# Token forms on VectorE, range sums on ScalarE, and another set of blocks in pairs, in a one-core decoder step on Trainium2

## The chip, the cores and the metric

The kernel runs on 1 core of one Trainium2 chip. A core has TensorE (PE in the profile; its weight loads are PEld), VectorE (DVE), ScalarE (ACT), GpSimd (POOL) and SyncE (SP), each with its own queue that it works off in order. Data come from HBM by DMA. The metric is the device time in microseconds of one execution, as the median of several; a profiled execution beside them gives the trace.

## The reference

One layer of a hybrid decoder is applied to 264 token columns (256 of a prompt, 8 single new tokens): a SwiGLU with half weight, a mixing block, a second SwiGLU, a last norm.

```
h = h + 0.5 * swiglu(rmsnorm(h, norm_ffn1), ffn1_gate, ffn1_up, ffn1_down)
mix = mixing_block(rmsnorm(h, norm_mix), w_in, ..., w_out, states)   # mLSTM heads | gated convolution
h = h + mix
h = h + 0.5 * swiglu(rmsnorm(h, norm_ffn2), ffn2_gate, ffn2_up, ffn2_down)
y = rmsnorm(h, norm_final)

def swiglu(x, wg, wu, wd):
    return (jax.nn.silu(x @ wg) * (x @ wu)) @ wd
```

`D_MODEL` is 2048 and `D_FF` 5504; all inputs are float32. Outputs are y and the new states of the mixing block.

## The kernel before

**Layout and precision.** Activations lie with channels on the 128 partitions and the 264 tokens along the row; 2048 channels are 16 blocks of 128, and 5504 are 43, split into a half 0 of 22 and a half 1 of 21. Every float32 operand is cut into a high and a low part of float16. ScalarE writes the high part (`high`, line 241), VectorE the low part (`low`, line 249). A regular product (`three`, lines 323 to 325) takes three matmuls of 264 columns for each 128x128 weight block: high by high, high by low, low by high.

**Weights.** `fetch` issues the DMA of a tile of up to 8 blocks (`wraw`), cuts its high part at once and its low part right away or, in the feed-forward parts (`lag`), with the next fetch. At most 5 tiles are cut ahead of TensorE.

**Pairs.** Some products are made two at a time (`product_pair`): gate and up of one block (key `gu`, table `GU_SEVEN`), or two columns of the down product (key `dd`, table `DOWN_SEVEN`). High by high stays as it is (line 387, 264 columns). The two correction terms are made in seven products of half the tokens (132 columns, lines 371 and 372) where eight would be needed. For that the kernel needs sums of weights (`weight_sums`, line 302, VectorE, four for each two tiles) and sums and differences of token halves, the "forms" (`token_sums`, line 359): `f` of the norm's output for gate/up, `g` of the activations for down. Before, GpSimd makes them, 4 instructions for two 128-channel blocks. Three banks of PSUM are joined afterwards (`join`, lines 427 to 437): ScalarE copies one piece, VectorE does the rest.

**What follows.** In gate/up, VectorE scales the result by the norm, ScalarE does SiLU, VectorE multiplies, and both cut the activation (`activated`). In the down products VectorE adds to h (line 872, or 855 for a joined pair). In half 1, `done` follows for each finished column: the next norm's cut (`xm`, both engines) and its square (GpSimd) in layer 1, the square and the last gain (line 919, ScalarE) in layer 2.

**Watching the range.** The float16 form is valid only for values in a range. `watch` (line 568) sums the absolute values of the last 16 columns of each regular product, on VectorE; a pair has its own sum (line 437). At the end a verdict is formed from them (`judge`), and a second, float32 form of the program would run if it failed.

**Order.** The schedule is written out by hand. `tick` counts products in halves, and `at(delta, fn)` puts work off by so many; what is put off stands in the engines' queues where its tick comes.

Of the kernel before, what the change touches and what calls it, by code (L numbers as in the profile page):

```python
# [8 lines left out]
F32 = mybir.dt.float32  # L9
# [3 lines left out]
AF = mybir.ActivationFunctionType  # L13
ALU = mybir.AluOpType
# [5 lines left out]
T = SEQ + NS  # L20
DFF = 5504
NFB = DFF // 128
HALVES = (range(0, 22), range(22, NFB))
# [5 lines left out]
WK = 8  # L29
# [7 lines left out]
SEEN = 16  # L37
# [13 lines left out]
GU_SEVEN = {  # L51
    n: [j for half in starts for j in half]
    for n, starts in (
        ("1", (range(7, 22, 5), range(9, 22, 5), range(22, NFB - 1, 5), range(24, NFB - 1, 5))),
        ("2", (range(5, 22, 5), range(7, 22, 5), range(22, NFB - 1, 5), range(24, NFB - 1, 5))),
    )
}
DOWN_SEVEN = {("1", 0): (1, 3, 5, 7), ("1", 1): (1, 3, 5, 6), ("2", 0): (1, 3, 5, 7), ("2", 1): (1, 3, 4)}
PAIRS = sum(len(v) for v in GU_SEVEN.values()) + sum(len(v) for v in DOWN_SEVEN.values())
TH = T // 2  # L60

# [104 lines left out]
def step(ctx: ExitStack, tc: tile.TileContext, a: dict, shared, bad=None):  # L166
    nc = tc.nc
    ident, beyond = shared
    PSUM = bass.MemoryType.PSUM
    half_size = bad is not None  # L170
    PART = F16 if half_size else F32R
# [4 lines left out]
    side = nc.gpsimd if half_size else nc.vector  # L176
# [12 lines left out]
    for kb in range(0, KB, 4):  # L189
        t = hpool.tile([128, 4, T], F32, name=f"h{kb}", tag=f"h{kb}")  # L190
# [104 lines left out]
    beside, sums, spool = [], [], [None]  # L295
# [12 lines left out]
    def at(delta, fn, *args):  # L308
        agenda.setdefault(int(seq[0]) + delta, []).append((fn, args))
# [37 lines left out]

    def token_sums(out, even, odd):  # L350

        left, right = slice(0, TH), slice(TH, T)
        for n, x, y, op in (
            (0, odd[:, :, left], odd[:, :, right], ALU.subtract),
            (1, even[:, :, right], odd[:, :, right], ALU.subtract),
            (2, out[:, 0], even[:, :, right], ALU.add),
            (3, even[:, :, left], out[:, 2], ALU.subtract),
        ):
            side.tensor_tensor(out[:, n], x, y, op=op)  # L359

    def product_pair(key, x, forms, order):

# [199 lines left out]
    def watch(ps, rows=None):  # L562

        if half_size:
            j, n = len(stats), ps.shape[-1]
            stats.append(j)
            for r in rows or [slice(0, 128)]:
                nc.vector.tensor_reduce(
                    stat[r, j : j + 1], ps[r, n - SEEN : n], axis=mybir.AxisListType.X,
                    op=ALU.add, apply_absolute_value=True,  # L570
                )

    def watch_norm(ssum):
# [102 lines left out]
    class Norm:  # L676


        def __init__(self, tag, col):
            self.tag, self.col, self.x, self.acc = tag, col, [None] * KB, None  # L680
            self.forms = []

        def block(self, kb):
            self.cut(kb)
            self.square(kb)

        def cut(self, kb):
            x = xpool.tile([128, 2, T], PART, tag=f"x{kb}", name=f"x{self.tag}{kb}")
            gain = gains[:, self.col + kb : self.col + kb + 1]
            if half_size and self.col == V_N1 and kb == 0:  # L690

                nc.vector.tensor_scalar(
                    x[:, 0, :], h[0], vecs[:, self.col : self.col + 1], sx, op0=ALU.mult,
                    op1=ALU.mult,
                )
                nc.vector.tensor_scalar_mul(gains, vecs[:, :V_FIN], sx)
                low(x[:, 1, :], h[0], x[:, 0, :], gain)
            else:
                split(x, h[kb], gain)
            self.x[kb] = x  # L700
            return x

        def form(self, k):
            t = self.fpool.tile([128, 4, 2, TH], PART, tag=f"f{k}", name=f"f{k}")
            token_sums(t, self.x[2 * k], self.x[2 * k + 1])
            self.forms.append(t)

        def square(self, kb):
            new = self.acc is None
# [7 lines left out]
        def square_pairs(self, pool, pairs):  # L717

            for i in pairs:
                sq = pool.tile([128, 2, T], F32, tag=f"f{i}", name=f"sq{i}")  # L720
                nc.scalar.activation(sq, hpair[i], AF.Square)
                if i == 0:
                    self.acc = sq
                elif half_size and i == 4:
                    self.more = sq
                elif half_size and i == 5:

                    side.tensor_tensor(self.more, self.more, sq, op=ALU.add)
                else:
                    nc.vector.tensor_tensor(self.acc, self.acc, sq, op=ALU.add)  # L730
                if half_size and i == KB // 2 - 1:
                    nc.vector.tensor_tensor(self.acc, self.acc, self.more, op=ALU.add)
# [25 lines left out]
    def ffn(layer, norm, done, start=None, end=None):  # L758
        with ExitStack() as stack:
# [11 lines left out]

            def activated(j, i, zu, sg):
                nc.vector.tensor_tensor(zu, zu, sg, op=ALU.mult)
                if i % 2 == 0:
                    couple[0] = apool.tile([128, 2, 2, T], PART, tag=f"a{i}", name=f"a{i}")
                act[j] = t = couple[0][:, i % 2]
                high(t[:, 0, :], zu, sa[layer])
                rest = t[:, 1, :], zu, t[:, 0, :], sa[layer]
                if lag[0] and j < blocks[-1] - 2:
                    at(1.5, low, *rest)  # L780
                else:
                    low(*rest)
                if half_size and i % 2:
                    at(2, act_form, i // 2, couple[0])

            couple, act_forms = [None], {}

            def act_form(n, pair):
                act_forms[n] = t = spool[0].tile([128, 4, 2, TH], PART, tag=f"g{n}", name=f"g{n}")
                token_sums(t, pair[:, 0], pair[:, 1])  # L790

            def by_seven(j, i):
                z, rest = join(product_pair((layer, "gu", j), norm.x, norm.forms, range(KB)))
# [14 lines left out]
            for half, blocks in enumerate(HALVES):  # L808
# [18 lines left out]
                for i, j in enumerate(blocks):  # L827
                    if j in sevens:
                        by_seven(j, i)
                        continue  # L830
                    if first and start is not None:

                        ps4 = start()
                        for n, ps in enumerate(ps4):
                            early[n // 2, "gu"[n % 2]] = ps
                        for step, pairs in ((0, (0, 1)), (1, (2, 3)), (1.5, (4, 5)), (2, (6, 7))):
                            at(step, norm.square_pairs, fpool, pairs)
                        tick(0)
                        for which in "gu":
                            early[2, which] = product((layer, which, 2), norm.x, range(KB))  # L840
                    if half_size and j == (3 if start is not None else 1):
                        for k in range(8):
                            at(1 + k / 2, norm.form, k)
                    lag[0] = half_size and j >= (3 if start is not None else 1)
                    if (j, "g") in early and not first:

                        at(j / 2 + 1, block, i, j)
                        continue
                    block(i, j)
# [3 lines left out]
                def joined(half, db, z, rest):  # L853
                    rest()
                    nc.vector.scalar_tensor_tensor(
                        hpair[db // 2], z, scale, hpair[db // 2], op0=ALU.mult, op1=ALU.add
                    )
                    if half == 1:
                        done(db)
                        done(db + 1)  # L860
                    if db // 2 == DOWN_SEVEN[layer, half][0]:
                        watch_tokens(z, 2 * (layer == "2") + half)

                for db in range(0, KB - apart, 2):
                    if half_size and db // 2 in DOWN_SEVEN[layer, half]:
                        forms = [act_forms[n] for n in range(len(blocks) // 2)]
                        ps = product_pair((layer, "dd", half, db), act, forms, list(blocks))
                        at(1, joined, half, db, *join(ps))
                        continue
                    for i in (db, db + 1):  # L870
                        ps = product((layer, "d", half, i), act, list(blocks))
                        nc.vector.scalar_tensor_tensor(
                            h[i], ps, scale, h[i], op0=ALU.mult, op1=ALU.add
                        )
                        if half == 1:
                            done(i)
                        watch(ps)
# [43 lines left out]
    def done(kb):  # L921
        nf.square(kb)
        gained(kb, slice(0, T))
# [767 lines left out]
```

## Time and profile before

| | |
|---|---|
| median of 3 runs | 1815.19 us (1814.66 to 1815.21) |
| the profiled execution | 1814.18 us, span 1812.5 us |
| granted TensorE clock | 0.997 |
| busy: PE, PEld | 1790.2 us, 1595.6 us |
| busy: DVE, ACT, POOL | 1535.5 us, 886.3 us, 402.5 us |
| moved by DMA | 381.48 MB, mean 210 GB/s |
| down products of layer 1, half 1 | 577 to 692 us |
| down products of layer 2, half 1 | 1683 to 1800 us |

A timeline row gives the start and the length in us, the engine, the line, what is written and read, and in brackets the engine's idle time before it and what ended that. A group row ends with busy time, the mean of one in ns, and the idle time before. A row of a stretch gives its two ends, its length and the busy time of PE, PEld, DVE, ACT and POOL, each with its count of instructions, then the clock, the DMA share and GB/s.

### The profile page before, as it was taken

How to read it: one execution, taken by the hardware profiler on the slowest of the kernel's cores; microseconds unless marked ns; L12 is line 12 of the kernel's file. 1: busy time of each engine (PE TensorE's matmuls, PEld its weight loads, DVE VectorE, ACT ScalarE, POOL GpSimd, SP SyncE). 2: the span in 40 equal slices, each digit the busy share in tenths (PEclk: the TensorE clock that was granted, in tenths of full speed). 3: DMA queues.
4: the chain of work that ended last, by engine and by line, in shares of the span. 5: the costliest groups of instructions: out<-in, count | busy, mean ns of one | idle time of the engine just before them, and what ended most of it. 6: DMA issues, size and time to landing. Idle time of an engine off the chain costs nothing.

```text
span 1812.5 us, 44544 instructions
## 1 busy us (share of the span) xinstructions
PE 1790.2 (99%) x18612; PEld 1595.6 (88%) x18612; DVE 1535.5 (85%) x2485; ACT 886.3 (49%) x1306; POOL 402.5 (22%) x432
## 2 busy tenths in 40 slices
PE   9999999999999999999999999999999999999997
PEld 7889988989998988888888888889989898898886
DVE  8999978888987998788888766889988898988685
ACT  7445444444444444667566645444444444444443
POOL 1921220011212122222121025612130001212221
PEclk9999999999999999999999999999999999999999
DMA  8666665666666556888887655666666666666554
GB/s 301 189 212 204 192 216 188 211 202 207 192 196 194 189 169 208 299 300 265 278 280 244 221 180 184 201 203 214 189 203 207 194 204 203 205 198 196 183 175 121
DMA packets 118514, 381.48 MB, mean 210 GB/s; under 512 B 14972, under 2 KB 24796, under 8 KB 118304
## 3 DMA queue, kind: packets, MB, share of 16 engines
q1 hardware_dynamic: 109104, 350.53, 60.4%
q0 software_dynamic: 8256, 27.57, 4.4%
q8 instruction: 147, 2.41, 0.5%
q14 instruction: 63, 0.52, 0.1%
q10 hardware_dynamic: 944, 0.45, 0.1%
HBM read 366.72 MB, written 11.78 MB: 209 GB/s over the span
## 4 chain that ended last, share of the span: by engine, by line
PE 90%; DVE 6%; DMA 1%; ACT 1%; issue 1%; POOL 0%; SPq 0%; DVEq 0%; ACTq 0%
PE ps L323 21%; PE ps L325 21%; PE ps L324 21%; PE ps L387 9%; PE ps L371 8%; PE ps L372 8%; DVE w L249 3%; DVE s L302 1%; DMA wraw<-in_w1gu 1%; ACT w L241 1%; PE ps L673 0%; PE ps L1360 0%; DMA h<-in_xt 0%; PE ps L1303 0%; ACT xm L241 0%
## 5 line engine op out<-in xcount | busy, mean ns | idle before, releaser
L249 DVE SCALAR_TENSOR_TENSOR w<-wraw,w 128x1024 f16<-128x1024 f32 (+3 forms) x692 | 829.1, 1223 | 92.4 <-ACT w L241 91.9
L241 ACT ACTIVATE w<-wraw 128x1024 f16<-128x1024 f32 (+3 forms) x692 | 670.1, 1007 | 204.0 <-PE ps L325 95.0
L323 PE MATMUL ps<-x,w 128*128 128x264 f16 x1760 | 485.8, 276 | 0.0
L324 PE MATMUL ps<-x,w 128*128 128x264 f16 x1760 | 485.8, 276 | 0.0
L325 PE MATMUL ps<-x,w 128*128 128x264 f16 x1760 | 485.8, 276 | 0.0
L325 PEld LDWEIGHTS <-w 128*128 128x128 f16 x3684 | 360.5, 98 | 54.7 <-DVE w L249 2.0
L324 PEld LDWEIGHTS <-w 128*128 128x128 f16 x3684 | 360.4, 98 | 54.0
L323 PEld LDWEIGHTS <-w 128*128 128x128 f16 x3684 | 360.8, 98 | 52.9 <-issue 0.6
L359 POOL TENSOR_TENSOR g<-a 128x264 f16<-128x264 f16 x84 | 109.7, 1325 | 827.9 <-DVE a L249 660.4
L323 PE MATMUL ps<-xm,w 128*128 128x264 f16 x896 | 247.3, 276 | 0.0
L325 PE MATMUL ps<-xm,w 128*128 128x264 f16 x896 | 247.3, 276 | 0.0
L324 PE MATMUL ps<-xm,w 128*128 128x264 f16 x896 | 247.3, 276 | 0.0
L325 PE MATMUL ps<-a,w 128*128 128x264 f16 (+2 forms) x772 | 204.4, 270 | 1.4 <-DVE w L249 1.4
L323 PE MATMUL ps<-a,w 128*128 128x264 f16 (+2 forms) x772 | 204.5, 270 | 0.0
L324 PE MATMUL ps<-a,w 128*128 128x264 f16 (+2 forms) x772 | 204.5, 270 | 0.0
L387 PEld LDWEIGHTS <-w 128*128 128x128 f16 x1574 | 151.4, 98 | 24.1 <-ACT w L241 2.9
L372 PEld LDWEIGHTS <-s 128*128 128x128 f16 x1560 | 151.8, 97 | 0.0
L371 PEld LDWEIGHTS <-s 128*128 128x128 f16 x1560 | 150.7, 97 | 0.1
L302 DVE TENSOR_TENSOR s<-s,w 128x1024 f16<-128x1024 f16 (+2 forms) x206 | 145.2, 705 | 3.6
L302 DVE TENSOR_TENSOR s<-w 128x1024 f16<-128x1024 f16 (+2 forms) x206 | 139.9, 720 | 4.1
L372 PEld LDWEIGHTS <-w 128*128 128x128 f16 x1184 | 115.8, 98 | 6.1 <-DVE w L249 4.4
L371 PEld LDWEIGHTS <-w 128*128 128x128 f16 x1184 | 115.5, 98 | 1.7
(271 smaller groups left out, 2335.5 us busy)
## 6 DMA issues: line engine op xcount, KB each, us to landing
wraw<-in_w2gu SPq DMA_DIRECT2D x172, 512.0 KB, 4.8
wraw<-in_w1gu SPq DMA_DIRECT2D x164, 512.0 KB, 4.7
wraw<-in_win SPq DMA_DIRECT2D x112, 512.0 KB, 5.6
wraw<-in_w2d SPq DMA_DIRECT2D x46, 448.0 KB, 3.9
wraw<-in_w1d SPq DMA_DIRECT2D x40, 512.0 KB, 4.5
wraw<-in_w2d SPq DMA_DIRECT2D x36, 512.0 KB, 4.5
wraw<-in_w1d SPq DMA_DIRECT2D x40, 448.0 KB, 4.0
wraw<-in_wout SPq DMA_DIRECT2D x32, 512.0 KB, 4.6
```

The source lines that it names most:

```text
L241: nc.scalar.activation(dst, src, AF.Copy, scale=scale)
L249: nc.vector.scalar_tensor_tensor(dst, src, scale, hi, op0=ALU.mult, op1=ALU.subtract)
L302: nc.vector.tensor_tensor(s[:, out], x, y, op=ALU.add)
L323: nc.tensor.matmul(ps, wh, xk[:, 0, :], start=first, stop=False)
L324: nc.tensor.matmul(ps, wh, xk[:, 1, :], start=False, stop=False)
L325: nc.tensor.matmul(ps, wl, xk[:, 0, :], start=False, stop=last)
L359: side.tensor_tensor(out[:, n], x, y, op=op)
L371: nc.tensor.matmul(ps, w[0], x[:, 1], start=first, stop=False)
L372: nc.tensor.matmul(ps, w[1], x[:, 0], start=False, stop=last)
L387: nc.tensor.matmul(ps[:, :T], hi[:, i], xs[i][:, 0], start=(k0 + i == 0), stop=False)
```

## The change

There are four edits. The tables change: gate/up pairs are every second block (35, before 29), and a half 1 has one down pair fewer in each layer (13 in all, before 15). `token_sums` runs on VectorE and takes eight blocks, four pairs, in one call of 4 instructions; for that x, the activations and the forms lie in tiles of eight blocks. `watch` runs on ScalarE as an Abs with a sum, into a scratch tile. And behind a joined down pair in half 1, `done` comes half a step and a whole step later, in place of at once.

```diff
 GU_SEVEN = {
...
-        ("1", (range(7, 22, 5), range(9, 22, 5), range(22, NFB - 1, 5), range(24, NFB - 1, 5))),
-        ("2", (range(5, 22, 5), range(7, 22, 5), range(22, NFB - 1, 5), range(24, NFB - 1, 5))),
+        ("1", (range(7, 21, 2), range(22, NFB - 1, 2))), ("2", (range(5, 21, 2), range(22, NFB - 1, 2))),
...
-DOWN_SEVEN = {("1", 0): (1, 3, 5, 7), ("1", 1): (1, 3, 5, 6), ("2", 0): (1, 3, 5, 7), ("2", 1): (1, 3, 4)}
+DOWN_SEVEN = {("1", 0): (1, 3, 5, 7), ("1", 1): (1, 3, 5), ("2", 0): (1, 3, 5, 7), ("2", 1): (1, 3)}
...
-    def token_sums(out, even, odd):
+    def token_sums(out, x):
...
-        for n, x, y, op in (
-            (0, odd[:, :, left], odd[:, :, right], ALU.subtract),
-            (1, even[:, :, right], odd[:, :, right], ALU.subtract),
-            (2, out[:, 0], even[:, :, right], ALU.add),
-            (3, even[:, :, left], out[:, 2], ALU.subtract),
+        even, odd = (x.rearrange("p (n e) s t -> p e n s t", e=2)[:, e] for e in (0, 1))
+        for n, a_, b_, op in (
+            (0, odd[:, :, :, left], odd[:, :, :, right], ALU.subtract),
+            (1, even[:, :, :, right], odd[:, :, :, right], ALU.subtract),
+            (2, out[:, 0], even[:, :, :, right], ALU.add),
+            (3, even[:, :, :, left], out[:, 2], ALU.subtract),
         ):
-            side.tensor_tensor(out[:, n], x, y, op=op)
+            nc.vector.tensor_tensor(out[:, n], a_, b_, op=op)
...
-                nc.vector.tensor_reduce(
-                    stat[r, j : j + 1], ps[r, n - SEEN : n], axis=mybir.AxisListType.X,
-                    op=ALU.add, apply_absolute_value=True,
+                seen = tmp.tile([128, SEEN], F32, tag="seen", name="seen", bufs=2)
+                nc.scalar.activation(
+                    seen[r], ps[r, n - SEEN : n], AF.Abs, accum_out=stat[r, j : j + 1]
                 )
...
-        def form(self, k):
-            t = self.fpool.tile([128, 4, 2, TH], PART, tag=f"f{k}", name=f"f{k}")
-            token_sums(t, self.x[2 * k], self.x[2 * k + 1])
-            self.forms.append(t)
+        def form(self, g):
+            t = self.fpool.tile([128, 4, 4, 2, TH], PART, tag=f"f{g}", name=f"f{g}")
+            token_sums(t, self.groups[g])
+            self.forms += [t[:, :, i] for i in range(4)]
...
-                if half_size and i % 2:
-                    at(2, act_form, i // 2, couple[0])
...
+                n = len(blocks) // 2 * 2
+                if half_size and i in (WK - 1, 2 * WK - 1, n - 1):
+                    at(2, act_form, g, groups[g][:, : min(WK, n - WK * g)])
...
-                        for k in range(8):
-                            at(1 + k / 2, norm.form, k)
+                        for g in range(2):
+                            at(1 + g, norm.form, g)
...
                     if half == 1:
-                        done(db)
-                        done(db + 1)
+                        at(0.5, done, db)
+                        at(1, done, db + 1)
```

How the queues change is shown at two places. The first is VectorE in layer 1, half 1, from the scaling of a regular block's up product (`tc`) to the join of the pair that follows it (`y`); `a` are activations, `w` weight cuts, `g` forms. Before, at blocks 28 (regular) and 29 (pair):

```order
L823 TENSOR_TENSOR tc<-ps,rstd 128x264
L773 TENSOR_TENSOR tc<-tc,tb 128x264
L568 TENSOR_REDUCE stat<-ps 128x1
L249 SCALAR_TENSOR_TENSOR w<-wraw,w 128x1024 x2
L249 SCALAR_TENSOR_TENSOR a_6148<-y_6319,a_6148 128x264
L249 SCALAR_TENSOR_TENSOR a_6468<-tc,a_6468 128x264
L249 SCALAR_TENSOR_TENSOR w<-wraw,w 128x1024 x2
L430 TENSOR_TENSOR y_6645<-y_6645,ps 128x132
```

Now, at blocks 29 (regular) and 30 (pair), where eight blocks of activations are complete:

```order
L837 TENSOR_TENSOR tc<-ps,rstd 128x264
L780 TENSOR_TENSOR tc<-tc,tb 128x264
L248 SCALAR_TENSOR_TENSOR w<-wraw,w 128x1024 x2
L248 SCALAR_TENSOR_TENSOR a_5621<-y_6506,a_5621 128x264
L248 SCALAR_TENSOR_TENSOR a_5621<-tc,a_5621 128x264
L248 SCALAR_TENSOR_TENSOR w<-wraw,w 128x1024
L359 TENSOR_TENSOR g_6751<-a_5621 128x1056 x2
L359 TENSOR_TENSOR g_6751<-g_6751,a_5621 128x1056
L359 TENSOR_TENSOR g_6751<-a_5621,g_6751 128x1056
L248 SCALAR_TENSOR_TENSOR w<-wraw,w 128x1024
L430 TENSOR_TENSOR y_6833<-y_6833,ps 128x132
```

The reduction is gone, and once in eight blocks four instructions of 1056 elements stand between two weight cuts, ahead of the next join.

The second place is ScalarE in layer 1, half 1, at the joined down pair of columns 10 and 11 (`y` is the join's copy, `xm` the next norm's input, `seen` the range sum). Before:

```order
L427 COPY y_9908<-ps 128x132
L241 ACTIVATE xm_9917<-h_82,gains 128x264
L241 ACTIVATE xm_9923<-h_82,gains 128x264
L241 ACTIVATE w<-wraw 128x640
L241 ACTIVATE w<-wraw 128x896 x5
L427 COPY y_10153<-ps 128x132
```

Now:

```order
L427 COPY y_10001<-ps 128x132
L240 ACTIVATE w<-wraw 128x896
L240 ACTIVATE xm_9667<-h_82,gains 128x264
L240 ACTIVATE w<-wraw 128x896 x2
L240 ACTIVATE xm_9667<-h_83,gains 128x264
L569 ACTIVATE seen,stat<-ps 128x16
L240 ACTIVATE xm_9667<-h_82,gains 128x264
L240 ACTIVATE w<-wraw 128x896 x3
```

A weight cut now stands ahead of the pair's first `xm`, two more ahead of its second, and a range sum follows the regular product of columns 12 and 13; before, that product was a pair as well.

More of the change, by code (lines that the diff above doesn't have):

```diff
@@ L680, in __init__ @@
             self.tag, self.col, self.x, self.acc = tag, col, [None] * KB, None
-            self.forms = []
+            self.forms, self.groups = [], []
         def block(self, kb):
@@ L687, in cut @@
         def cut(self, kb):
-            x = xpool.tile([128, 2, T], PART, tag=f"x{kb}", name=f"x{self.tag}{kb}")
+            g, i = kb // WK, kb % WK
+            if i == 0:
+                self.groups.append(
+                    xpool.tile([128, WK, 2, T], PART, tag=f"x{g}", name=f"x{self.tag}{g}")
+                )
+            x = self.groups[g][:, i]
             gain = gains[:, self.col + kb : self.col + kb + 1]
@@ L719, in square_pairs @@
             for i in pairs:
-                sq = pool.tile([128, 2, T], F32, tag=f"f{i}", name=f"sq{i}")
+                if i % 4 == 0:
+                    self.four = pool.tile([128, 4, 2, T], F32, tag=f"f{i // 4}", name=f"sq{i}")
+                sq = self.four[:, i % 4]
                 nc.scalar.activation(sq, hpair[i], AF.Square)
@@ L773, in activated @@
                 nc.vector.tensor_tensor(zu, zu, sg, op=ALU.mult)
-                if i % 2 == 0:
-                    couple[0] = apool.tile([128, 2, 2, T], PART, tag=f"a{i}", name=f"a{i}")
-                act[j] = t = couple[0][:, i % 2]
+                g = i // WK
+                if i % WK == 0:
+                    groups[g] = apool.tile(
+                        [128, min(WK, len(HALVES[0]) - i), 2, T], PART, tag=f"a{g}", name=f"a{g}"
+                    )
+                act[j] = t = groups[g][:, i % WK]
                 high(t[:, 0, :], zu, sa[layer])
@@ L782, in activated, with act_form @@
                     low(*rest)
-                if half_size and i % 2:
-                    at(2, act_form, i // 2, couple[0])
[L786 to L790, printed above, removed]
+                n = len(blocks) // 2 * 2
+                if half_size and i in (WK - 1, 2 * WK - 1, n - 1):
+                    at(2, act_form, g, groups[g][:, : min(WK, n - WK * g)])
+            groups, act_forms = {}, {}
+            def act_form(g, x):
+                n = x.shape[1] // 2
+                room = min(WK, len(HALVES[0]) - WK * g) // 2
+                t = spool[0].tile([128, 4, room, 2, TH], PART, tag=f"g{g}", name=f"g{g}")[:, :, :n]
+                token_sums(t, x)
+                act_forms[g] = [t[:, :, i] for i in range(n)]
             def by_seven(j, i):
@@ L865, in ffn @@
                     if half_size and db // 2 in DOWN_SEVEN[layer, half]:
-                        forms = [act_forms[n] for n in range(len(blocks) // 2)]
+                        forms = [x for g in range(3) for x in act_forms[g]]
                         ps = product_pair((layer, "dd", half, db), act, forms, list(blocks))
```

## The prediction

> **What bounds the kernel now.** I read the page first, then TensorE's timeline and its waits, then the queues of ScalarE and VectorE around each wait.
>
> ```profile
> span 1812.5 us, 44544 instructions
> PE 1790.2 (99%) x18612; PEld 1595.6 (88%) x18612; DVE 1535.5 (85%) x2485; ACT 886.3 (49%) x1306; POOL 402.5 (22%) x432
> PE 90%; DVE 6%; DMA 1%; ACT 1%; issue 1%; POOL 0%; SPq 0%; DVEq 0%; ACTq 0%
> ```
>
> TensorE is busy 99%, but the page says that a matmul's end is modelled, so the price of a matmul has to come from starts. These are the starts in layer 1, half 1: block 27 (a pair), block 28 (regular), block 29 (a pair).
>
> ```profile
> 408.80 1.96 PE L387 MATMUL ps<-x,w 128*128 128x264 f16 x16
> 410.60 0.22 PE L371 MATMUL ps<-x,w 128*128 128x132 f16 x1
> ...
> 413.82 1.96 PE L387 MATMUL ps<-x,w 128*128 128x264 f16 x16
> ...
> 418.84 0.28 PE L323 MATMUL ps<-x,w 128*128 128x264 f16 x1
> ...
> 429.64 1.96 PE L387 MATMUL ps<-x,w 128*128 128x264 f16 x16
> 434.66 1.96 PE L387 MATMUL ps<-x,w 128*128 128x264 f16 x16
> ```
>
> 16 matmuls of 264 columns take 410.60 - 408.80 = 1.80 us, 112.5 ns each; the 56 of 132 columns after them take 413.82 - 410.60 = 3.22 us, 57.5 ns each. The pair takes 10.04 us (408.80 to 418.84), the regular block 10.80 us (418.84 to 429.64). So TensorE is bound by its own stream here, and what it does not spend there it loses at a few places:
>
> ```profile
> 673.59 0.29 PE L372 MATMUL ps<-a,w 128*128 128x264 f16 x1 [3.25 <-DVE w L249]
> 674.88 0.40 PE L372 MATMUL ps<-a,w 128*128 128x264 f16 x1 [0.32 <-DVE w L249]
> 1751.73 0.74 PE L387 MATMUL ps<-a,w 128*128 128x264 f16 x5 [2.62 <-ACT w L241]
> 1755.18 0.29 PE L325 MATMUL ps<-a,w 128*128 128x264 f16 x1 [0.37 <-DVE w L249]
> 1772.90 0.29 PE L325 MATMUL ps<-a,w 128*128 128x264 f16 x1 [1.01 <-DVE w L249]
> ```
>
> All five lie in the down products of a half 1. The first two are in the pair of columns 12 and 13 of layer 1, the third in the pair of columns 8 and 9 of layer 2, the last two just behind that one. They add up to 7.57 us of idle time. A matmul's modelled 0.276 us overlaps its successor by 0.276 - 0.1125 = 0.16 us, which the idle time does not count, so the loss is nearer to 7.57 + 5 x 0.16 = 8.4 us. Why they happen stands in the other queues:
>
> ```profile
> 659.67 0.27 ACT L427 COPY y<-ps 128x132 f32<-128x132 f32 x1 [0.19 <-PE ps L372]
> 670.44 0.92 ACT L241 ACTIVATE xm<-h,gains 128x264 f16<-128x264 f32 x2 [10.51 <-DVE h L855]
> 671.27 4.08 ACT L241 ACTIVATE w<-wraw 128x640 f16<-128x640 f32 x5
> 1738.32 0.27 ACT L427 COPY y<-ps 128x132 f32<-128x132 f32 x1 [0.36 <-PE ps L372]
> 1749.13 0.52 ACT L919 ACTIVATE h<-h,vecs 128x264 f32<-128x264 f32 x1 [10.54 <-POOL sq L711]
> 1750.95 4.92 ACT L241 ACTIVATE w<-wraw 128x640 f16<-128x640 f32 x6
> 1747.18 0.70 DVE L855 SCALAR_TENSOR_TENSOR h<-y,h 128x528 f32<-128x528 f32 x1
> ```
>
> After a joined pair ScalarE's next work is the follow-up of that pair's columns (L241 into xm, L919 into h). It needs h of L855, which VectorE reaches only when its backlog is done: ScalarE stands for 10.5 us, with five or six weight tiles to be cut right behind. Both times the next product was a pair too.
>
> **The TensorE stream.** Gate/up pairs go from 29 to 35, down pairs from 15 to 13. A regular block has 96 matmuls of 264 columns; a pair has 32 of 264 and 112 of 132. Six more pairs: 6 x (10.80 - 10.04) = 4.56 us less. Both lost down pairs are in a half 1, with 21 blocks: two regular products are 126 x 112.5 ns = 14.18 us, a pair is 46 x 112.5 + 140 x 57.5 = 13.23 us; two of them cost 1.90 us. The stream gets shorter by **2.66 us**.
>
> **The five waits.** The two pairs in which TensorE waits are just the ones that become regular, and `done` moves behind the joined pair by half a step and a step, so the weight cut at each of those points goes ahead of it. Layer 2's remaining products after column 7 are all regular, so its verdict work (L625 and on, before the 1.01 us wait) meets a VectorE that has had four products more to get ahead. I take all 8.4 us as gone. The other end is that they are passed on to the next product whole, 0 us; I am near the first because three earlier pairs of layer 1's half 1 and two of layer 2's show no wait in this trace, with the same follow-up.
>
> **VectorE, which now makes the forms.** What it gains and loses, from these rows:
>
> ```profile
> L249 DVE SCALAR_TENSOR_TENSOR w<-wraw,w 128x1024 f16<-128x1024 f32 x556 | 696.1, 1273 | 71.1 <-ACT w L241 70.8
> L302 DVE TENSOR_TENSOR s<-s,w 128x1024 f16<-128x1024 f16 x176 | 130.5, 741 | 3.0
> L302 DVE TENSOR_TENSOR s<-w 128x1024 f16<-128x1024 f16 x176 | 126.3, 758 | 3.6
> L568 DVE TENSOR_REDUCE stat<-ps 128x1 f32<-128x16 f32 x220 | 36.1, 164 | 0.0
> L359 POOL TENSOR_TENSOR g<-a 128x264 f16<-128x264 f16 x84 | 109.7, 1325 | 827.9 <-DVE a L249 660.4 <-PE ps L372 126.9 <-DVE stat L568 40.5
> 409.49 1.29 DVE L302 TENSOR_TENSOR s<-w 128x1024 f16<-128x1024 f16 x2
> 415.90 2.36 DVE L249 SCALAR_TENSOR_TENSOR w<-wraw,w 128x1024 f16<-128x1024 f32 x2
> 437.67 3.28 DVE L249 SCALAR_TENSOR_TENSOR w<-wraw,w 128x1024 f16<-128x1024 f32 x2
> 408.80:429.64 20.84, 20.84 (x243) 18.96 (x241) 18.52 (x30) 9.07 (x14) 0.00 (x0) 1.00 0.67 203
> 429.64:450.48 20.84, 20.84 (x243) 18.97 (x241) 18.90 (x28) 10.50 (x14) 4.54 (x4) 1.00 0.67 210
> ```
>
> In the last two rows the columns are TensorE, weight loads, VectorE, ScalarE and GpSimd. In the first stretch GpSimd is idle; in the second it makes one form set (4.54 us), and two weight cuts of VectorE take 3.28 us there instead of 2.36. No row has VectorE making a form. The nearest by kind and type is a sum of weights, f16 into f16 of 1024 elements, 0.645 us; for 1056 that is 0.665 us, 2.7 us for a set of four. If the cut-up input cost it the faster rate, the nearest row is the low cut at 1.18 us per 1024, so 1.22 and 4.9 us. I take 0.665: the sums read cut-up inputs too. The forms are worth 58 instructions of 1056, 39 us (71 at the upper end). A pair and a regular block now need 18.52 - 2 x 0.16 (the reductions go) + 2.7/4 = 18.9 us of VectorE, against 20.84 us of TensorE. Over the whole run: +39 forms, +18 sums (32 more of 1024, 8 fewer of 512), +8 joins, -36 reductions, and about -70 where GpSimd had slowed its neighbours (696.1 - 556 x 1.18 = 40 for the low cuts, 130.5 + 126.3 - 352 x 0.645 = 30 for the sums): VectorE ends near 1495 us. Nothing of it is on the path as long as VectorE stays ahead. How far ahead it is:
>
> ```profile
> 432.12 1.41 DVE L302 TENSOR_TENSOR s<-s,w 128x1024 f16<-128x1024 f16 x2
> 419.34 0.29 DVE L430 TENSOR_TENSOR y<-y,ps 128x132 f32<-128x132 f32 x1 [1.08 <-ACT y L427]
> 429.65 1.23 DVE L249 SCALAR_TENSOR_TENSOR w<-wraw,w 128x1024 f16<-128x1024 f32 x1 [0.30 <-ACT w L241]
> ```
>
> Sums for block 29's second half end at 433.53; TensorE starts that half at 434.66, and reads the first sum after 16 matmuls of 264 and three terms of 8 of 132, 434.66 + 1.80 + 1.38 = 437.84: 4.3 us ahead. A set of forms stands in the queue once in eight blocks, so 1.6 us remain even if nothing else gives. If that cover were gone, each of the 16 sets would show, at up to 2.7 us.
>
> **ScalarE, which now makes the range sums.**
>
> ```profile
> L1311 ACT ACTIVATE den<-ps 128x1 f32<-128x1 f32 x8 | 1.4, 171 | 8.8 <-PE ps L1303 8.8
> L1451 ACT ACTIVATION_READ_ACCUMULATOR jk<-jk 128x1 f32 x64 | 12.1, 189 | 0.0
> ```
>
> 214 of them at 0.17 + 0.19 = 0.36 us are 77 us on an engine busy 49%; its order has no table load more than before. Each waits for VectorE's read of the same bank, and SiLU or the next weight cuts queue behind it. In gate/up SiLU waited for that read before; so it adds 0.36 us per product, not a wait. In the mixing projections and the first half's downs the wait is new, but four or five tiles (2.7 us each on TensorE) are cut ahead there. I take 0 for it; the other end is the slower rival.
>
> **The sum.** The profiled execution took 1814.18 us. 1814.18 - 2.66 - 8.4 = 1803.1. The median of the three runs, 1815.19, lies 1.0 above that execution, so the forecast is **1804.1 us**, with 1802 to 1806.5 as its own range (small waits one way, the wait before the mixing block and at the start, 2 us in all, the other).
>
> **Rivals.** *The waits move on.* Columns 10 and 11 of layer 1 stay a pair, on a VectorE with little lead, and ScalarE has more in front of its cuts. One or two waits like the 3.25 us stay: 1804.1 + 4 = 1808. *All of them move on:* only the stream is left, 1815.19 - 2.66 = 1812.5, within the 0.2% (3.6 us) that a measurement here can tell from no change. *VectorE becomes the bound in the gate/up stretches (slower).* Of 20.84 us it idles 2.32 now. If all of that were forced, and the two range sums (0.72 us) came on top, two blocks would take 18.9 + 2.32 + 0.72 = 21.9 us; 1.1 us over TensorE, 35 times, less a lead of 4.3 us used up in each of four stretches, is 21 us: 1825. It decides from a forced idle time of 1.2 us on. For it: the waits for ScalarE's cuts (0.30 in the row above) are in series. Against it: 1.08 us of the 2.32 ended with ScalarE's copy of y, which TensorE's end released (that is, VectorE was early), and this vanishes when VectorE is late. *Weight loads show (slower).* Were a 98 ns weight load not hidden behind a 132-column matmul, 392 more of those and 224 fewer of 264 would cost 392 x 98 - 224 x 112.5 ns = +13.2 us instead of -2.66: 1820.
>
> ```profile
> L372 PEld LDWEIGHTS <-s 128*128 128x128 f16 x1560 | 151.8, 97 | 0.0
> ```
>
> The 57.5 ns from starts speak against it. [...] The trace has 57.5 ns for 132 columns, and it decides.
>
> **Chances.** Forecast 0.70; waits move on in part 0.17 (up to 1811.5); in full 0.06; VectorE or ScalarE the bound 0.06; weight loads 0.01. So faster by over 0.2% 0.87, within 0.06, slower 0.07. The range takes in the first case and most of the second: 1801.5 to 1810.
>
> **What will show it.** Starts in a pair: 10.04 us again. No PE wait over 0.5 us between 600 us and 690 us or after 1730 us, apart from the last verdict. GpSimd near 140 us busy, its L359 rows gone; a form of 1056 near 0.67 us; low cuts of 1024 all near 1.2 us; VectorE near 1495 us, ScalarE near 960. I am wrong if TensorE waits on w or s in blocks 22 to 42, or if waits appear at columns 8 to 13 of a half 1.

## The result, and the profile after

The changed kernel takes 1838.74 us (median of 4 runs, 1836.0 to 1840.74) against 1814.93 us (1814.46 to 1815.21) for the kernel before beside it: a ratio of 1.013, 95% interval 1.0113 to 1.0148. It is slower by 24 us where 1804.1 us was forecast, and no rival came near 1838. Slow executions are left out of all times here (one of e5's ten, at 3815 us, and one of the kernel before, at 1857 us).

These lines of the page answer to the first ones of the prediction (the span, the busy time by engine, the chain by engine):

```profile
span 1838.5 us, 44896 instructions
PE 1798.1 (98%) x18780; PEld 1600.2 (87%) x18780; DVE 1525.3 (83%) x2371; ACT 912.0 (50%) x1738; POOL 140.4 (8%) x200
PE 74%; DVE 11%; ACT 7%; issue 5%; DMA 1%; SPq 0%; ACTq 0%; DVEq 0%; POOL 0%; POOLq 0%
```

No engine has become full. Yet the chain of waits, which was 90% TensorE, is now 74% TensorE and 18% VectorE and ScalarE. Something passes from one to the other and back. The table shows where: for each stage the time from its first matmul to the next stage's first, as a difference to the kernel before, for the changed kernel and for the experiments whose verdict hangs on it (the table is worked out from the matmuls' starts in the traces).

| stage | before | after | e1 | e2 | e3 | e5 | e7 | e8 | e11 | e12 |
|---|---|---|---|---|---|---|---|---|---|---|
| layer 1, end of the opening | 12.6 | -0.9 | -0.1 | +0.6 | +0.8 | +2.9 | +0.2 | +0.1 | +1.3 | +0.3 |
| layer 1, gate/up, half 0 | 200.7 | +3.7 | +0.2 | +0.3 | +2.3 | +0.6 | +10.1 | +0.1 | +0.8 | +3.9 |
| layer 1, gate/up, half 1 | 220.7 | -1.1 | -1.5 | 0.0 | -1.0 | +0.1 | +3.0 | -1.5 | -1.5 | -1.0 |
| layer 1, downs, half 1 | 117.7 | -4.8 | -4.8 | -0.1 | -4.9 | -1.2 | -4.9 | -4.9 | -4.8 | -4.9 |
| mixing projections | 333.7 | **+31.8** | 0.0 | **+28.1** | +1.6 | 0.0 | +0.7 | **+25.9** | -0.1 | +8.1 |
| output projection | 86.4 | +2.0 | 0.0 | +2.0 | 0.0 | 0.0 | 0.0 | +1.5 | 0.0 | 0.0 |
| layer 2, gate/up, half 0 | 232.7 | -0.3 | -0.8 | +0.1 | -0.3 | +0.1 | +8.6 | -0.7 | -0.7 | -0.3 |
| layer 2, gate/up, half 1 | 220.7 | -1.1 | -1.5 | +0.1 | -1.0 | 0.0 | +3.0 | -1.5 | -1.5 | -0.8 |
| layer 2, downs, half 1 | 129.4 | -3.7 | -3.8 | +0.4 | -3.7 | -4.5 | -3.9 | -3.8 | -4.0 | -3.8 |

The downs of both halves 0 stay within 0.1 us everywhere. So the changed kernel gains about 12 us in the feed-forward layers and loses 33.8 us in the mixing projections and the start of the output projection, and 3.7 us near the start of layer 1. All five waits that the prediction named are gone. These are TensorE's waits over the whole run now (us in total, times, longest):

```profile
PE ps L673 <- ACT sq L1473: 13.3, 4, 5.3
PE ps L324 <- DVE w L248: 6.6, 10, 2.3
PE ps L322 <- ACT w L240: 2.5, 2, 2.3
PE ps L1000 <- DVE ok L994: 2.3, 1, 2.3
PE ps L323 <- DVE xa L248: 1.8, 1, 1.8
```

The largest is no wait for weights: TensorE wants column sums of the heads' squares (L673), and ScalarE is late with the squares (L1473). Between 692 and 1068 us the starts that come over 0.25 us late add up to some 26 us. In three stretches behind the longer of these waits the granted clock is 0.50, and the matmuls there lose another 7.6 us (both worked out from the starts); together that is about the 33.8 us. What ScalarE and VectorE wait for in the mixing projections, first before, then after:

```profile
DVE w L249 <- ACT w L241: 24.1, 17, 3.4
ACT w L241 <- PE ps L325: 22.7, 13, 2.9
...
ACT ht L1336 <- DVE rt L1333: 19.9, 4, 5.0
```

```profile
DVE w L248 <- ACT w L240: 75.7, 48, 3.4
ACT seen L569 <- DVE qkv L1036: 74.0, 24, 7.6
...
ACT seen L569 <- DVE ta L1036: 30.2, 8, 5.3
...
ACT seen L569 <- DVE tb L1036: 19.5, 8, 3.2
...
ACT seen L569 <- DVE zo L1036: 12.8, 7, 4.4
...
ACT seen L569 <- DVE tc L1036: 3.5, 4, 1.6
```

Before, ScalarE's longest wait was for TensorE to give weight buffers back (L325): it was as far ahead as the buffers let it. Now it stands for 140 us at the new range sums (L569), each time until VectorE has made its product from the same bank (L1036); and VectorE's own waits for ScalarE's weight cuts have grown from 24.1 to 75.7 us. (The 133 us that an expectation below names leave out the stage's last 21 us.) One round of it, from the timeline of the changed kernel (start, length, engine and line, what is written and read, idle time before):

```profile
862.91 0.42 DVE L1036 TENSOR_TENSOR qkv<-ps,rstd 128x264 f32<-128x264 f32 x1
...
863.43 0.18 ACT L569 ACTIVATE seen<-ps 128x16 f32<-128x16 f32 x1 [4.35 <-DVE qkv L1036]
...
865.51 1.99 ACT L240 ACTIVATE w<-wraw 128x1024 f16<-128x1024 f32 x2
...
866.59 2.36 DVE L248 SCALAR_TENSOR_TENSOR w<-wraw,w 128x1024 f16<-128x1024 f32 x2 [3.25 <-ACT w L240]
...
871.05 0.42 DVE L1036 TENSOR_TENSOR qkv<-ps,rstd 128x264 f32<-128x264 f32 x1
871.57 0.18 ACT L569 ACTIVATE seen<-ps 128x16 f32<-128x16 f32 x1 [4.07 <-DVE qkv L1036]
...
875.60 0.20 ACT L1473 ACTIVATE sq<-ha 128x16 f32<-128x16 f32 x1
...
875.85 0.38 PE L673 MATMUL ps<-sq,ones 128*128 128x8 f32 x1 [5.33 <-ACT sq L1473]
```

VectorE ends its product at 863.33; only then does ScalarE go on, with 1.9 us of other work and then the weight cut that VectorE needs next. VectorE stands for 3.25 us, cuts, does its work for the heads, and reaches the next product 8.1 us after the last. A projection is 48 matmuls, 5.4 us of TensorE. Two queues that each work in order have been tied together, and in this round one sleeps while the other works. ScalarE's squares, queued behind the second sum and 3.9 us of other work, come 5.3 us late. Over the whole stage the two engines have as much to do as before (VectorE 271 us against 277, ScalarE 220 against 214), but both are at work at once for 142 us in place of 173 (worked out from the starts and ends of their instructions). That is 32 us less side by side, in a stage that is 31.8 us longer.

### The profile page after: what moved, and what is told of

Its sections match the earlier page's. It is cut to its first block, busy times and chain, and to the rows that moved or that the text cites. A ratio compares the mean times of both kernels' runs of the same rounds, so it can differ in the third digit from the quotient of the medians.

```text
span 1838.5 us, 44896 instructions
## 1 busy us (share of the span) xinstructions
PE 1798.1 (98%) x18780; PEld 1600.2 (87%) x18780; DVE 1525.3 (83%) x2371; ACT 912.0 (50%) x1738; POOL 140.4 (8%) x200
## 4 chain that ended last, share of the span: by engine, by line
PE 74%; DVE 11%; ACT 7%; issue 5%; DMA 1%; SPq 0%; ACTq 0%; DVEq 0%; POOL 0%; POOLq 0%
PE ps L324 16%; PE ps L322 16%; PE ps L323 16%; PE ps L387 10%; PE ps L371 8%; PE ps L372 8%; DVE w L248 4%; ACT w L240 3%; DVE s L301 1%; ACT jk L1465 1%; DMA wraw<-in_w1gu 1%; ACT cs L1437 1%; ACT seen L569 1%; DVE jk L1457 0%; DVE qkv L1036 0%
## 5 line engine op out<-in xcount | busy, mean ns | idle before, releaser
L248 DVE SCALAR_TENSOR_TENSOR w<-wraw,w 128x1024 f16<-128x1024 f32 (+3 forms) x692 | 800.6, 1181 | 159.6 <-ACT w L240 158.3
L324 PE MATMUL ps<-x,w 128*128 128x264 f16 x1568 | 433.6, 277 | 3.3 <-DVE w L248 3.3
L322 PE MATMUL ps<-x,w 128*128 128x264 f16 x1568 | 433.6, 277 | 0.0
L323 PE MATMUL ps<-x,w 128*128 128x264 f16 x1568 | 433.5, 276 | 0.0
L324 PEld LDWEIGHTS <-w 128*128 128x128 f16 x3576 | 350.8, 98 | 63.7 <-DVE w L248 9.6
L322 PEld LDWEIGHTS <-w 128*128 128x128 f16 x3576 | 351.3, 98 | 55.1 <-ACT w L240 3.0
L323 PEld LDWEIGHTS <-w 128*128 128x128 f16 x3576 | 350.9, 98 | 53.4 <-issue 0.3
L322 PE MATMUL ps<-a,w 128*128 128x264 f16 (+2 forms) x856 | 227.7, 271 | 0.0
L323 PE MATMUL ps<-a,w 128*128 128x264 f16 (+2 forms) x856 | 227.7, 271 | 0.0
L324 PE MATMUL ps<-a,w 128*128 128x264 f16 (+2 forms) x856 | 227.6, 271 | 0.0
L569 ACT ACTIVATE seen<-ps 128x16 f32<-128x16 f32 (+1 forms) x214 | 37.5, 175 | 331.3 <-DVE ta L831 132.2
L387 PEld LDWEIGHTS <-w 128*128 128x128 f16 x1682 | 162.0, 98 | 22.8
L372 PEld LDWEIGHTS <-s 128*128 128x128 f16 x1672 | 162.2, 97 | 0.0
L371 PEld LDWEIGHTS <-s 128*128 128x128 f16 x1672 | 161.3, 96 | 0.0
L387 PE MATMUL ps<-x,w 128*128 128x264 f16 x1120 | 137.4, 276 | 0.0
L372 PEld LDWEIGHTS <-w 128*128 128x128 f16 x1264 | 123.3, 98 | 1.7
```

The costliest lines, as they stand in the source:

```text
L248: nc.vector.scalar_tensor_tensor(dst, src, scale, hi, op0=ALU.mult, op1=ALU.subtract)
L322: nc.tensor.matmul(ps, wh, xk[:, 0, :], start=first, stop=False)
L323: nc.tensor.matmul(ps, wh, xk[:, 1, :], start=False, stop=False)
L324: nc.tensor.matmul(ps, wl, xk[:, 0, :], start=False, stop=last)
L371: nc.tensor.matmul(ps, w[0], x[:, 1], start=first, stop=False)
L372: nc.tensor.matmul(ps, w[1], x[:, 0], start=False, stop=last)
```

## The experiments

Theory L (lockstep): the range sum on ScalarE must wait for VectorE's read of its bank, ScalarE loses its lead over VectorE in the mixing projections, and the two take turns. Rival W: ScalarE has too much work of its own. Rival F: the forms on VectorE make it late.

### Who makes the sums, and where: e1, e2, e3, e4

e1 is the changed kernel with the sums back on VectorE:

```
-                seen = tmp.tile([128, SEEN], F32, tag="seen", name="seen", bufs=2)
-                nc.scalar.activation(
-                    seen[r], ps[r, n - SEEN : n], AF.Abs, accum_out=stat[r, j : j + 1]
-                )
+                nc.vector.tensor_reduce(
+                    stat[r, j : j + 1], ps[r, n - SEEN : n], axis=mybir.AxisListType.X,
+                    op=ALU.add, apply_absolute_value=True,
+                )
```

> The changed kernel with the range sums back on VectorE everywhere; tables, forms and the later done stay. Theory L (lockstep: a range sum on ScalarE waits for VectorE's read of the same bank, so that ScalarE can no longer run ahead in the mixing projections): the 33.8 us between 692 and 1060 us go, the 3.6 us at 57 us stay in part: 1804 to 1808 us. Rival W (ScalarE has too much work of its own with 0.36 us for each of 214 sums): the same here. Rival F (the forms on VectorE make it late): 1832 to 1840 us.

e2 makes the opposite edit, alone, in the kernel before.

> The kernel before with nothing but the range sums moved to ScalarE. L: the loss of the mixing block comes alone, 25 to 35 us: 1840 to 1850 us, with the range sums waiting for VectorE's reads for over 100 us between 690 and 1040 us. W: the same time. F: 1813 to 1817 us.

e3 swaps two lines of the changed kernel:

```
     def project(b, out=None, tag="ta"):
         ps = product(("in", b), nm.x, all_k)
         z = out if out is not None else t264(tag)
+        watch(ps)
         nc.vector.tensor_tensor(z, ps, nm.r, op=ALU.mult)
-        watch(ps)
```

> The changed kernel, but in the mixing projections the range sum stands ahead of VectorE's read of the bank: the same 56 sums on ScalarE, which now wait for TensorE alone, and VectorE's read waits for them. L: most of the 33.8 us goes: 1804 to 1812 us, and ScalarE's waits for VectorE's reads are gone there. W: ScalarE does the same work, so 1832 to 1840 us. F: 1832 to 1840 us.

e4 gives only that one call of `watch` back to VectorE.

> The changed kernel with the range sums of the mixing projections alone back on VectorE (the other 158 stay on ScalarE). L: the loss sits in these 56, so 1804 to 1809 us; if the gate/up, down and output blocks lose by it as well, more than e1 by what they lose. W: some 20 of the 77 us of work go from ScalarE, and those in the stretch that lost: 1805 to 1815 us. F: 1832 to 1840 us.

| | time, us | ratio to before (95%) |
|---|---|---|
| e1, all sums on VectorE | 1802.45 | 0.9937 (0.992 to 0.9953) |
| e2, before, sums on ScalarE | 1845.62 | 1.0176 (1.0159 to 1.0193) |
| e3, sum ahead of VectorE's read | 1807.88 | 0.9966 (0.9952 to 0.998) |
| e4, 56 sums on VectorE | 1807.17 | 0.9964 (0.9951 to 0.9976) |

e1 comes 1.6 us below the range given for it. F is out: e1 keeps the forms on VectorE and is fast, e2 has none there and is slow. W is out too: e3 leaves the same 56 sums on ScalarE, at the same work, and gives back 31 us. e4 does not tell L from W, whose ranges overlap there. e2 and e1 differ from their kernels by the sums alone, +31.3 us (1845.62 - 1814.31) and -36.3 us (1838.74 - 1802.45). In e3 the sums wait for the product of TensorE (first row), not for VectorE; in e2 they wait as in the changed kernel (second row, 136 us with its four smaller rows):

```profile
ACT seen L569 <- PE ps L324: 66.3, 33, 4.5
```

```profile
ACT seen L569 <- DVE qkv L1022: 71.5, 24, 7.6
```

A wait of 66 us in e3 costs 1.6 us in its stage, one of 140 us in the changed kernel costs 31.8. The difference is whom ScalarE waits for. TensorE sets the end anyway, so a ScalarE that waits for TensorE is early; one that waits for VectorE is tied to VectorE's delays. ScalarE's weight cuts end a median of 9.7 us before TensorE starts their tile in the mixing projections of the kernel before, 9.3 us in e3, 7.5 us in the changed kernel, where the worst is 0.06 us (2.65 before).

Why there is a wait at all: the read of a bank that comes second in the program waited for the first here. In the round shown above, of the changed kernel, ScalarE's sum starts 0.10 us after VectorE's product has ended (863.33 to 863.43); in e9, where the sum comes first, VectorE's product stands 0.65 us for it (at 43.91 us). No run here tried it without the wait; what was free to choose was the order.

### The wait by itself, and shortened: e8, e12

e8 leaves the sums with VectorE, as e1, and adds a small copy on ScalarE that waits for VectorE's product and reads no bank:

```
         nc.vector.tensor_tensor(z, ps, nm.r, op=ALU.mult)
         watch(ps)
+        late = tmp.tile([128, SEEN], F32, tag="late", name="late", bufs=2)
+        nc.scalar.copy(late, z[:, T - SEEN :])
```

> e1_watch_vector, and behind each of the 56 mixing projections ScalarE copies 16 columns of VectorE's product into a tile that nobody reads: a wait for VectorE with about 0.17 us of work, and no reading of PSUM by ScalarE. Theory L (the wait alone costs it): 1827 to 1838 us, with TensorE's waits for the heads' squares of some 5 us again. If the price was the reading of a bank by both engines, or the 0.36 us of work: 1802 to 1808 us.

It takes 1831.45 us (1.01 of before, 1.0083 to 1.0117): 29.0 us more than e1. The waits come back, and TensorE's wait for the squares with them (the sum on VectorE stands right behind its product, so most waits are put down to it):

```profile
ACT late L1039 <- DVE stat L568: 84.5, 31, 5.3
...
ACT late L1039 <- DVE qkv L1036: 33.7, 10, 7.7
...
PE ps L673 <- ACT sq L1475: 10.9, 3, 5.2
```

So neither the bank nor the sum's own time is the main price: a copy that does nothing but wait for VectorE's newest product makes 25.9 of the stage's 31.8 us. What the other 5.9 us are is not shown.

e12 puts the sums of the changed kernel one product later into ScalarE's queue (`at(1, watch, ps)` in place of `watch(ps)`).

> The changed kernel with each range sum of the mixing projections put one product (5.4 us of TensorE) later into ScalarE's queue; it still waits for VectorE's read of its bank, and is the same work. Theory L with its place: ScalarE runs some 2.5 us ahead of VectorE there (median lead over TensorE at a weight tile 9.8 us against 7.3 us in e1_watch_vector), so a product later the read is done and the wait is short: 1805 to 1811 us, ScalarE's waits for VectorE's products under 40 us in place of 133. If ScalarE only falls behind by as much again, or the banks held longer stop TensorE: 1815 to 1838 us.

It takes 1816.11 us (1.0004, 0.9995 to 1.0014), the lower end of what the second case would give, and not L's 1805 to 1811. The waits are halved, not gone:

```profile
ACT seen L569 <- DVE qkv L1036: 26.9, 12, 7.6
ACT seen L569 <- DVE ta L1036: 15.2, 6, 4.8
ACT seen L569 <- DVE tb L1036: 13.2, 5, 3.1
```

With the smaller rows (6.3, 3.4 and 1.4) that is 66 us against 140, and the stage's loss falls from 31.8 to 8.1 us. Some of VectorE's products come more than a projection behind ScalarE: a wait of 7.6 us is left. Another 1.6 us of the distance to L's range lie in layer 1's first gate/up stretch (+3.9 us here, +2.3 in e3), where the two do not differ. The loss grows faster than the wait. ScalarE does not get its lead back in e12, where the median is 7.1 us. What shrinks is the waits for the squares, which no weight cut ahead can cover:

```profile
PE ps L673 <- ACT sq L1473: 4.0, 3, 1.7
```

They were 13.3 us in the changed kernel, and what the clock of 0.50 costs in the stage falls with them, from 7.6 to 1.5 us. VectorE and ScalarE work at once for 165 us here, between the 142 and the 173.

### What the rest of the change does: e5, e6, e7, e11

e1 stands for the change without its sums. From it e5 takes the new tables out, e6 the later `done`, and e7 gives the forms to GpSimd (still four pairs at once: `side.tensor_tensor` for `nc.vector.tensor_tensor` in `token_sums`). e11 is the kernel before with nothing but the tables.

> e1_watch_vector (the changed kernel with the range sums on VectorE) with the two tables of the kernel before: 29 gate/up blocks and 15 down pairs go by seven products. The stream of TensorE is 2.66 us longer by the prediction's sum, and nothing else changes if the later done alone took the waits out of the second halves' downs: 1804 to 1806.5 us. If the tables (one down pair fewer in each second half) took them out, up to 8.4 us come back: 1809 to 1814 us, with waits at the downs' ends.

> e1_watch_vector with the two done calls back at once behind a joined pair of the second halves. If the later done took the waits of 8.4 us out: 1807 to 1811 us, with waits of TensorE near 660 and 1745 us. If the tables or the forms did: 1801 to 1804 us.

> e1_watch_vector with the forms of four pairs at once made by GpSimd instead of VectorE. If it makes no difference who makes them, 1800 to 1804 us: VectorE has 44 us less of its own, and its low cuts take again 1.22 us instead of 1.18. If GpSimd's load was what made VectorE late in the second halves' downs, waits come back there: 1805 to 1811 us. The first pair of each layer may wait for the forms, which come later by GpSimd: up to 3 us.

> The kernel before with nothing but the two new tables (35 gate/up blocks, 13 down pairs): the forms stay with GpSimd, one pair at a time, the range sums with VectorE, done at once. TensorE's stream is 2.66 us shorter by the prediction's sum; e5_old_tables against e1_watch_vector says that the tables also take most of the waits out of the second halves' downs: 1803 to 1807 us. If these waits need the forms on VectorE as well to go: 1808 to 1812 us.

| | time, us | ratio to before (95%) |
|---|---|---|
| e5, e1 with the old tables | 1810.53 | 0.9976 (0.9966 to 0.9986) |
| e6, e1 with `done` at once | 1802.01 | 0.9934 (0.9918 to 0.9951) |
| e7, e1 with the forms on GpSimd | 1830.58 | 1.009 (1.0073 to 1.0107) |
| e11, before with the tables alone | 1803.13 | 0.9931 (0.9915 to 0.9947) |

The tables alone do all that can be measured: e11 and e1 lie 0.7 us apart, and their ranges overlap. Against e1, e5 loses 8.1 us, more than the 2.66 us of the stream. In its profiled execution 3.6 us lie in layer 1's downs of half 1, where waits of 0.4 to 0.9 us on w and s are left in and just behind the pair of columns 12 and 13, the one that the new table takes out; and 3.0 us lie in the opening, ahead of any pair, where the two programs do not differ and the wait for the norm's sums comes out longer (2.6 us in e5, 0.6 us in e1). The later `done` is worth nothing beside the new tables. Forms and later `done` together gain 3.9 us under the old tables (e5 against before), most of it in layer 2's downs (-4.5 us); these runs do not separate the two there.

e7 is the miss: I had expected 1800 to 1811 us. A form set of four pairs on GpSimd lasts 10.8 us (207.31 to 218.1), and two weight cuts of VectorE that start beside it last 6.12 us instead of 2.36. From the timeline of e7:

```profile
207.31 5.16 POOL L359 TENSOR_TENSOR g<-a 128x1056 f16<-128x1056 f16 x2 [76.53 <-DVE a L248]
...
207.43 6.12 DVE L248 SCALAR_TENSOR_TENSOR w<-wraw,w 128x1024 f16<-128x1024 f32 x2
```

In the kernel before, beside GpSimd's instructions of 264 columns, two such cuts took 3.28 us. TensorE's waits in e7 name no form; most of them are for weight cuts, above all VectorE's:

```profile
PE ps L324 <- DVE w L248: 12.7, 12, 2.5
```

So the forms can be made by GpSimd in small pieces (e11) or by VectorE in large ones (e1), at the same time for the kernel; by GpSimd in large ones they cost 28 us.

### The remainder: e9, e10

e4 and e3 lie 5 us above e1. e9 is e3 with the sum ahead of VectorE's read in the regular gate/up blocks too.

> e3_watch_first, and in the regular gate/up blocks too the range sum stands ahead of VectorE's read of its bank. e3 still lies 5.4 us above e1_watch_vector: in its profile 2.4 us in the first gate/up stretch (a wait of 2.6 us at 57 us where e1 has 1.0), 0.5 us in each other, 1.6 us in the mixing projections. If waits for VectorE's reads make this remainder too: 1802.5 to 1805 us. If the 0.36 us of work of each sum make it: 1806 to 1809 us. VectorE now waits for ScalarE's sum in each block: if that is the worse coupling, above 1809 us.

It takes 1806.79 us (0.995, 0.9934 to 0.9965). The four waits of about 0.45 us behind the form sets are gone, and all later gate/up stretches are as short as in e1. What is left against e1 is 3.4 us in layer 1's first gate/up stretch and 2.6 us in the mixing projections. The 3.4 us are one place: TensorE waits 2.6 us at 60 us where e1 has 0.8, and behind it the clock is 0.50 for 3.4 us, which costs 1.7 us. So the waits for VectorE's reads made a small part of the remainder, 1.1 us by the medians of different comparisons, and the time lies in the range given for the sums' work. That it is the work is not shown by it: VectorE now waits for the sums in turn. What makes that wait longer than e1's, and what the 2.6 us are, stays open. In the opening, of the changed kernel too, the form sets stand ahead of a weight cut that TensorE is about to read (from the timeline of the changed kernel):

```profile
55.32 1.32 DVE L359 TENSOR_TENSOR f<-x 128x1056 f16<-128x1056 f16 x2
...
56.56 0.70 DVE L359 TENSOR_TENSOR f<-f,x 128x1056 f16<-128x1056 f16 x1
...
57.29 0.71 DVE L359 TENSOR_TENSOR f<-x,f 128x1056 f16<-128x1056 f16 x1
57.92 1.22 DVE L248 SCALAR_TENSOR_TENSOR w<-wraw,w 128x1024 f16<-128x1024 f32 x1
...
59.19 0.29 PE L324 MATMUL ps<-x,w 128*128 128x264 f16 x1 [2.29 <-DVE w L248]
```

In e1 the same wait is 0.8 us long. e10 is e1 with the two sets put later, `at(3 + 3 * g, norm.form, g)` in place of `at(1 + g, norm.form, g)`.

> e1_watch_vector with the two sets of forms of a layer's inputs put 3 and 6 products behind the start of its gate/up blocks instead of 1 and 2, where VectorE's low cuts have more lead. The wait of 1.0 us at 56 us should go, and nothing else change: 1800.5 to 1802.5 us. If the sets then stand in front of the first pair's range of sums: 1802.5 to 1806 us.

It takes 1801.06 us (1800.37 to 1803.92; ratio 0.9924, 0.991 to 0.9938). The wait is gone, and that stretch is 1.0 us shorter than in e1, as expected; between the medians of e10 and e1, which come from different comparisons, 1.4 us is no more than the runs scatter. Its median is the lowest here, and below that of both kernels. TensorE's longest waits in it are the last verdict, the start and the norm's sums:

```profile
PE ps L1000 <- DVE ok L994: 2.3, 1, 2.3
PE idle L212 <- DVE ones L202: 1.1, 1, 1.1
PE ps L673 <- DVE sq L739: 1.1, 1, 1.1
```

## Why the prediction was wrong, point by point

**The step that failed** is in the part on ScalarE: "In the mixing projections and the first half's downs the wait is new, but four or five tiles (2.7 us each on TensorE) are cut ahead there. I take 0 for it; the other end is the slower rival." For the downs 0 is right. In the mixing projections it was 25.9 us for the wait alone (e8), and 31.8 us with the sums. Two things were wrong in the reasoning. First, tiles cut ahead are a stock, and I treated them as if they covered the wait each time; a wait that comes back with every one of 56 products, longer than the slack of that product, empties the stock and then shows. The stretch needed an account of both queues together. With ScalarE at 215 us and VectorE at 279 us of 336, as the first row below shows for the kernel before, either fits beside TensorE; together they are 494 us, so for at least 158 us both must be at work at once. The changed kernel has nearly the same work there (second row), and the wait takes 32 us of working at once away.

```profile
692.00:1028.00 336.00, 335.62 (x2931) 290.28 (x2929) 278.92 (x561) 215.04 (x418) 63.14 (x101) 1.00 0.79 265
```

```profile
692.00:1058.00 366.00, 344.18 (x2890) 293.34 (x2886) 271.29 (x497) 220.74 (x527) 55.85 (x100) 0.98 0.71 236
```

(TensorE, weight loads, VectorE, ScalarE and GpSimd, then clock, DMA share and GB/s; the second row is the changed kernel.) Second, the cover was the wrong one for half of it. ScalarE's squares go to TensorE at once; no tile cut ahead covers these, and 13.3 of TensorE's 22 us of waits in the stage are there, the longest of 5.3 us.

And "the other end is the slower rival" gave no price to this place: that rival was worked out for the gate/up stretches, at 1825 us, where SiLU had waited for VectorE before anyway. There the prediction holds: ScalarE's longest wait by name, 132 us at the sums of the gates, is no loss in the later gate/up stretches beyond 0.5 us each (after against e1).

```profile
L569 ACT ACTIVATE seen<-ps 128x16 f32<-128x16 f32 x212 | 37.2, 175 | 331.2 <-DVE ta L831 132.2 <-DVE qkv L1036 74.0 <-DVE h L886 53.7
```

The mechanism was named in the text; it was priced in the wrong place.

**The stream.** Right. A pair and a regular block now go from 401.27 to 422.11, 20.84 us, as before:

```profile
401.27 1.96 PE L387 MATMUL ps<-x,w 128*128 128x264 f16 x16
...
422.11 1.96 PE L387 MATMUL ps<-x,w 128*128 128x264 f16 x16
```

The gate/up stretches of e1 are shorter by 1.5, 0.8 and 1.5 us, the two halves 1 as two pairs more make them (2 x 0.76).

**The five waits.** Right in size: the downs of half 1 are 4.8 and 3.7 us shorter, though two pairs fewer make their own stream 1.9 us longer: 4.8 + 3.7 + 1.9 = 10.4 us where 8.4 were expected. The sum had left out the clock: behind the 3.25 us wait of the kernel before it is 0.50 from 674.7 to 678.1 us, which costs about 1.6 us by the starts, and that went with the wait. The cause was half right: that the pairs become regular is enough (e11), and the later `done`, which I gave as the second reason, adds nothing (e6).

**VectorE and the forms.** Right that they cost nothing in the steady stretches; the size of a form was near:

```profile
L359 DVE TENSOR_TENSOR g<-a 128x1056 f16<-128x1056 f16 x16 | 10.6, 700 | 0.0
L248 DVE SCALAR_TENSOR_TENSOR w<-wraw,w 128x1024 f16<-128x1024 f32 x548 | 658.8, 1223 | 140.6 <-ACT w L240 139.6
```

0.70 us instead of 0.665 us. VectorE ends at 1525 us instead of 1495, mostly because a low cut takes 1.22 us by its row where I had 1.18. Wrong in the opening of layer 1, which I had not looked at for this: 1.0 us there in e1, and the wait of 2.29 us with its aftermath in the changed kernel, where the sums on ScalarE add to it (e4 has that wait too, e1 only 0.8 us of it).

**ScalarE's work.** I had 77 us for the 214 sums; busy time rose by 25.7 us. The read of the accumulator overlaps the activation (it starts at 863.51, 0.08 us behind it), and the next instruction follows a sum's start after 0.18 us (863.43 to 863.61), not 0.36. The sums bring no table load, as said: ScalarE has 18 before and after.

**The sum.** Without the sums on ScalarE it came out: 1802.45 us (e1) and 1803.13 us (e11) against 1804.1 us. Of the rivals, *the waits move on* and *weight loads show* did not happen: no wait over 0.5 us is left in the downs, apart from the verdict, and a pair takes its old time. GpSimd is at 140.4 us, as said.

## What to carry to other kernels

Before an instruction goes to another engine's queue, list what it will wait for there: if it is the newest result of a third engine, the two queues can be tied to each other at every repetition (e8: 29.0 us), and busy shares of 49% and 85% say nothing of it. Check the sum of the two engines' busy times in that stretch against its length, and what else stands behind the waiting instruction, above all what is wanted at once. If both must read one bank, put the reader that runs ahead first (e3: 31 us for the order of two lines), or leave the work with the engine that is already there.

## What the runs showed of the hardware

The wait of TensorE of 2.29 us that ends at 59.19 us in the changed kernel cost more than itself. Stretches around it (TensorE's busy time first, the granted clock third from the end):

```profile
56.00:59.20 3.20, 0.92 (x10) 0.56 (x7) 3.17 (x6) 1.91 (x3) 0.00 (x0) 1.00 0.02 8
59.20:60.10 0.90, 0.90 (x8) 0.79 (x9) 0.90 (x2) 0.00 (x0) 0.00 (x0) 0.97 0.00 0
60.10:63.00 2.90, 2.90 (x15) 1.98 (x13) 2.87 (x6) 1.54 (x5) 0.00 (x0) 0.50 0.79 210
```

Here the clock falls to 0.50 at 60.04 us, 0.85 us after work has begun again, and for about 3 us the matmuls of 264 columns start 220 ns apart, 107 ns more than usual. It fell behind all the waits of over 5 us in the mixing projections of the changed kernel (5.33 and 5.25 us), e2 (the longest 5.3 us) and e8 (the longest 5.2 us); behind the one that ends at 875.85 us in the changed kernel it stayed at 0.50 for 6.8 us, in which 23 matmuls of 264 columns lost 2.5 us. Behind shorter waits it varies. It fell after waits of 2.3 to 2.6 us in e7, e9 and e12, and after one of 1.7 us in e12 (at 808 us), but not after those of 2.5 us in e3 and e4, at the same place in the program as e9's, nor after the one of 2.62 us at 1751 us in the kernel before. Behind waits of 0.86 and 1.56 us in the changed kernel (at 794 and 752 us) and of 1.01 us in the kernel before (at 1773 us) it stayed at 1.00. The stretches at 0.50 within the runs last 3.4 or 6.8 us. What tells waits of like length apart was not shown.

VectorE's cuts lasted longest beside GpSimd's long instructions: two cuts took 6.12 us beside instructions of 1056 columns (e7), 3.28 us beside those of 264 (the kernel before), 2.36 us alone. Over the whole run a low cut of 1024 took 1.333 us in e7 and 1.222 us in e1, the same kernel with the forms on VectorE. e7 lies 27 us above e11, where the same forms are made in small pieces. TensorE's waits in e7 are mostly for weight cuts (12.7 us for VectorE's) and none for a form, which points at the stretched cuts; how much of the 27 us is theirs was not measured apart.
